# Issuing a kernel's weight loads from GpSimd instead of SyncE

## The chip, the cores and the metric

The kernel runs on one core of a Trainium2 chip. The metric is device time in microseconds (us) of one execution; the time of a version is the median of its runs. The engines are TensorE (PE in the profile; its weight loads are PEld), VectorE (DVE), ScalarE (ACT), GpSimd (POOL) and SyncE (SP). SPq and ACTq are the queues that issue DMA transfers.

## The reference

One layer of a hybrid decoder on 256 tokens of width 2048, all in float32:

```
h = rmsnorm(x) * norm_mix_w;  proj = h @ w_in            # q, k, v, z, b, a, p, g_a, g_b
q, k, v = silu(causal_conv4(q, k, v)); q, k normalised
o  = gated_delta_rule(q, k, v, decay(a), sigmoid(b))     # 16 heads of 128, chunks, triangular solve
y_a = rmsnorm(o) * silu(z);  y_b = (pool(p) - p) @ pool_w * pool_scale
x  = x + (sigmoid(g_a) * y_a + sigmoid(g_b) * y_b) @ w_out
gate, up = split(rmsnorm(x) @ w_up)                      # 2 x 5632
x  = x + (gelu(causal_conv3(gate) + b) * up) @ w_down
y  = rmsnorm(x) * norm_final_w
```

## The kernel before

Every large product is made of weight tiles: 256 rows by 512 columns of a weight matrix, which are 128 partitions x 2 x 512 floats, 512 KB. The list `srcs` holds all 530 of them in the order of their use. `w_in` and the small `pool_w` come in four groups of heads with 512 columns each, then `w_out`, `w_up` and `w_down`. The two tiles with the columns of b and a are cut otherwise, 128 x 8 x 128.

Each tile goes through three steps. `fetch` loads it into one of five raw buffers (`RAWS = 5`); `cast` on ScalarE rounds it to a short float format as `whi`; `split` on VectorE subtracts that from the raw tile and leaves the rest as `wlo`. The raw buffer is free after the split. `whi` and `wlo` have four buffers each, so three tiles can stand made ahead (`AHEAD = 3`). Then TensorE runs 12 products of 128 x 512 for the tile: eight with `whi`, four with `wlo`. The time goes through the mixer with its four groups (until about 720 us), the output projection, the up projection (about 810 to 1285) and the down projection.

Beside this main line run side chains, written as generators: turning a block (a transpose of 32 x 32 squares on VectorE into `tn`, four `flip` stores to DRAM and one load back, as `kq`, `vT`, `pu`, `gs`, `us`, `mlo` or `fhl`; `back` and `vt` are the way back for v), the decays (`rund` to `dec`, cut on GpSimd), and the inversion of a triangular matrix for each group (`cd` copied on GpSimd, `cdd` and `lb` as transfers, 31 steps on VectorE that make `tb`, then `tbd`, `tct`, the matrices `T` and `TT`, and small products into `psa`). SyncE issues all of these and all weight loads; ScalarE issues a few loads of vectors.

Nothing is scheduled by the compiler: the order on each engine is the order in which the Python program emits the instructions. A small model, `Plan`, guides it. It keeps a time for each engine (`t`, with keys PE, V, A, G, S), and `pipeline` emits the next split, cast or fetch when the model's time for the engine has come to what the step needs (`soon`). The side chains get their turns from `piece` by the same times. On the chip an engine executes in that order and waits by semaphore at each instruction; what is behind a waiting instruction on the same engine waits too. `matrices`, at the start, makes constants on GpSimd.

Of the kernel before, what the change touches and what calls it, by code (L numbers as in the profile page):

```python
# [14 lines left out]
S = 256  # L15
# [13 lines left out]
RAWS = 5  # L29


class Plan:
# [17 lines left out]
    def dma(self, eng, out):  # L50
        n = 4
        for d in out.shape:
            n *= d
        self.t[eng] = max(self.t[eng], self.base) + (0.42 if eng == "S" else 0.1)
        self.queue = max(self.queue, self.t[eng]) + n / (170e3 if out.shape[-1] <= 32 else 380e3)
        self.ready = max(self.ready, self.queue + 2.0)

# [50 lines left out]
def kernel(  # L108
# [22 lines left out]
    nc = Engines(plan, tc.nc)  # L131
# [12 lines left out]
    def nm(s):  # L144
        cnt[0] += 1
        return f"{s}_{cnt[0]}"
# [92 lines left out]
    def side():  # L239
        ready = plan.ready  # L240
        count = 0
        while True:
            step = None if piece(-99, min(taken[0] - (19 if taken[0] else 20), -3), 4.0) else pipeline()
            if step:
                step()
            elif not piece(-99, 9):
                break
            count += 1
        plan.at(ready)
        return count  # L250
# [11 lines left out]
    srcs = []  # L262
# [25 lines left out]
    free = []  # L288
# [3 lines left out]
    def soon(eng, time):  # L292
        return time <= max(now["PE"], now[eng])
# [8 lines left out]
    def fetch():  # L302
        i = len(raws)
        src = srcs[i]
        raw = wpool.tile(list(src.shape), F32, tag="raw", name=nm("raw"), bufs=RAWS)
        plan.at(free[i - RAWS] if i >= RAWS else 0.0)
        nc.sync.dma_start(raw, src)
        landed.append(plan.ready)
        raws.append(raw)

# [23 lines left out]
    def pipeline():  # L334
        i = len(made)
        if i < len(rounded) and soon("V", cast_at[i]):
            return split
        i = len(rounded)
        if i < min(len(raws), taken[0] + AHEAD) and soon("A", landed[i]):
            return cast  # L340
        i = len(raws)
        if i < min(len(srcs), len(free) + RAWS) and soon("S", free[i - RAWS] if i >= RAWS else 0.0):
            return fetch
        return None

    def weights():
        n = taken[0]
        taken[0] += 1
        side()
        for done, step in ((raws, fetch), (rounded, cast), (made, split)):  # L350
            while len(done) <= n:
                step()
        plan.at(max(cast_at[n], free[n] - 1.8))
        return made[n]
# [76 lines left out]
    for c in range(4):  # L431
        xc = mtile(c, [P, 2, 512], F32, f"x0_{c}")
        plan.at(0.0)
        nc.sync.dma_start(xc, x[0, :, c * 512 : (c + 1) * 512].rearrange("(t p) d -> p t d", p=P))
        x0.append((xc, plan.ready))
        fetch()
# [989 lines left out]
```

## Time and profile before

| what | us |
|---|---|
| median of three runs (1532.01 to 1534.3) | 1533.48 |
| profiled execution, own time | 1536.53 |
| its span, first to last instruction | 1533.5 |
| TensorE busy | 1519.9 |
| VectorE busy | 1059.4 |
| ScalarE busy | 775.4 |
| GpSimd busy | 62.5 |

The profiled execution is one more than the three runs. Busy time counts instructions and not the issuing of transfers, for which the queues' rows (SPq) stand. A TensorE row's end is modelled, and products overlap in the pipeline, so that 12 products of 390 ns each take 2.72 us.

### The profile page before, as it was taken

The page shows a single profiled execution, that of the slowest core. Times are in us where ns is not written, and L with a number is a line of the kernel's source. Part 1 is how long each engine was busy: PE and PEld are TensorE (multiplying, and loading weights), DVE is VectorE, ACT ScalarE, POOL GpSimd, SP SyncE. Part 2 cuts the span into 40 slices and gives each one's busy share as a digit, 9 for nine tenths or more (in the row PEclk, how much of TensorE's full clock was granted, in tenths as well). Part 3 has the DMA queues.
Part 4 walks back from the last instruction along what each step waited for, and adds up shares of the span by engine and source line. Part 5 has one row for each costly group of instructions (what it writes and reads, how often), then busy time and mean ns, then how long its engine had stood idle before and what let it go on. Part 6 is the DMA issues. An engine that isn't in the chain of part 4 may idle for free.

```text
span 1533.5 us, 19655 instructions
## 1 busy us (share of the span) xinstructions
PE 1519.9 (99%) x7110; PEld 1250.0 (82%) x7110; DVE 1059.4 (69%) x1525; ACT 775.4 (51%) x1023; POOL 62.5 (4%) x85
## 2 busy tenths in 40 slices
PE   9999999999999999999999999999999999999997
PEld 8887888777878887888888888888888888888886
DVE  5767878787887779885566766666666666444445
ACT  7475474466545854464455544444454444333343
POOL 1001001100010002000000000000000000000000
PEclk9999999999999999999999999999999999999999
DMA  8888975898578966974798888877887788666663
GB/s 292 224 238 219 256 243 149 206 260 256 159 178 245 288 201 167 264 230 143 228 281 270 235 255 245 258 220 242 253 248 227 237 255 240 204 193 192 220 194 108
DMA packets 399271, 346.09 MB, mean 226 GB/s; under 512 B 231190, under 2 KB 258374, under 8 KB 399174
## 3 DMA queue, kind: packets, MB, share of 16 engines
q1 hardware_dynamic: 395744, 339.32, 75.3%
q10 hardware_dynamic: 3430, 5.53, 1.1%
q8 instruction: 55, 0.90, 0.2%
q14 instruction: 42, 0.34, 0.1%
HBM read 315.40 MB, written 29.39 MB: 225 GB/s over the span
## 4 chain that ended last, share of the span: by engine, by line
PE 93%; DMA 3%; DVE 2%; issue 1%; SPq 0%; ACT 0%; POOLq 0%; POOL 0%; ACTq 0%; DVEq 0%
PE psm L94 79%; PE psa L94 8%; PE psb L94 6%; DMA raw<-in_w_in_dram 2%; DVE wlo L94 1%; DMA lb<-cdd 0%; DMA pu<-flip 0%; SPq L94 0%; DVE tmp L94 0%; ACT whi L94 0%; DVE tb L94 0%; DMA flip<-tn 0%; ACT xt L94 0%; DVE pb L94 0%; DVE tn L94 0%
## 5 line engine op out<-in xcount | busy, mean ns | idle before, releaser
L94 DVE TENSOR_TENSOR wlo<-raw,whi 128x1024 fp32r<-128x1024 f32 x524 | 635.2, 1220 | 293.1 <-ACT whi L94 291.4
L94 ACT CAST whi<-raw 128x1024 fp32r<-128x1024 f32 x526 | 549.0, 1051 | 536.9 <-PE psm L94 360.7
L94 PE MATMUL psm<-whi,xhl 128*128 128x512 f32 x1792 | 452.7, 393 | 1.4 <-ACT whi L94 1.4
L94 PEld LDWEIGHTS psm<-whi,xhl 128*128 128x128 f32 x1792 | 335.4, 188 | 71.6 <-ACT whi L94 2.2
L94 PE MATMUL psm<-whi,fhl 128*128 128x512 f32 x1408 | 347.8, 389 | 0.0
L94 PEld LDWEIGHTS psm<-whi,fhl 128*128 128x128 f32 x1408 | 264.5, 188 | 54.7
L94 PE MATMUL psm<-wlo,xhl 128*128 128x512 f32 x896 | 243.4, 394 | 0.6 <-DVE wlo L94 0.6
L94 PEld LDWEIGHTS psm<-wlo,xhl 128*128 128x128 f32 x896 | 167.4, 188 | 35.6 <-DVE wlo L94 1.1
L94 PE MATMUL psm<-wlo,fhl 128*128 128x512 f32 x704 | 188.3, 389 | 0.0
L94 PEld LDWEIGHTS psm<-wlo,fhl 128*128 128x128 f32 x704 | 132.2, 188 | 27.3
L94 PE MATMUL psm<-whi,hhi 128*128 128x512 f32 x168 | 65.4, 389 | 0.0
L94 PE MATMUL psm<-whi,hlo 128*128 128x512 f32 x168 | 65.4, 389 | 0.0
L94 ACT ACTIVATE fev<-psm,rs 128x512 f32<-128x512 f32 x44 | 27.9, 686 | 55.3 <-PE psm L94 55.3
L94 DVE STREAM_TRANSPOSE tn<-fev 128x1024 f32<-128x1024 f32 x22 | 27.4, 1244 | 32.3 <-ACT fev L94 32.1
L94 DVE SCALAR_TENSOR_TENSOR cy<-kq,cqw,cy 128x255 f32<-128x255 f32 (+2 forms) x96 | 44.5, 481 | 1.6
L94 PE MATMUL psm<-wlo,hhi 128*128 128x512 f32 x168 | 45.2, 389 | 0.0
L94 DVE SCALAR_TENSOR_TENSOR y<-gs,cfw,y 128x255 f32<-128x255 f32 x88 | 42.6, 484 | 3.1
L94 DVE TENSOR_TENSOR tmp<-lb,tb 128x248 f32<-128x248 f32 (+30 forms) x124 | 36.5, 294 | 10.1 <-DMA lb<-cdd 7.3
L94 DVE TENSOR_TENSOR tb<-tb,tmp 128x248 f32<-128x248 f32 (+30 forms) x124 | 36.9, 298 | 4.3
L94 POOL TENSOR_TENSOR rs<-ms,epsx 128x2 f32<-128x2 f32 (+1 forms) x4 | 4.2, 1062 | 822.0 <-DVE ms L94 822.0
L94 PE MATMUL psm<-whi,mhi 128*128 128x512 f32 x96 | 37.4, 389 | 0.0
L94 PE MATMUL psm<-whi,mlo 128*128 128x512 f32 x96 | 37.4, 389 | 0.0
(223 smaller groups left out, 1288.4 us busy)
## 6 DMA issues: line engine op xcount, KB each, us to landing
raw<-in_w_in_dram SPq DMA_DIRECT2D x226, 512.0 KB, 5.3
raw<-in_w_up_dram SPq DMA_DIRECT2D x176, 512.0 KB, 4.5
raw<-in_w_down_dram SPq DMA_DIRECT2D x88, 512.0 KB, 4.6
flip<-tn SPq DMA_DIRECT2D x184, 128.0 KB, 3.2
raw<-in_w_out_dram SPq DMA_DIRECT2D x32, 512.0 KB, 5.1
gs<-flip SPq DMA_DIRECT2D x11, 512.0 KB, 5.5
us<-flip SPq DMA_DIRECT2D x11, 512.0 KB, 6.2
kq<-flip SPq DMA_DIRECT2D x8, 512.0 KB, 8.2
```

What stands on the lines that cost most here:

```text
L94: r = getattr(self.eng, op)(out, *args, **kw)
```

## The change

Three lines. The model charges 1.0 us for a load on GpSimd (it was 0.1 for every engine but SyncE); a tile from the sixth on is issued by GpSimd; and a fetch is emitted when GpSimd's time, not SyncE's, has come to the moment at which its buffer is free.

```diff
@@ Plan.dma
-        self.t[eng] = max(self.t[eng], self.base) + (0.42 if eng == "S" else 0.1)
+        self.t[eng] = max(self.t[eng], self.base) + dict(S=0.42, G=1.0).get(eng, 0.1)
@@ fetch
         plan.at(free[i - RAWS] if i >= RAWS else 0.0)
-        nc.sync.dma_start(raw, src)
+        (nc.gpsimd if i >= RAWS else nc.sync).dma_start(raw, src)
@@ pipeline
-        if i < min(len(srcs), len(free) + RAWS) and soon("S", free[i - RAWS] if i >= RAWS else 0.0):
+        if i < min(len(srcs), len(free) + RAWS) and soon("G", free[i - RAWS] if i >= RAWS else 0.0):
```

SyncE before, in the second group of heads (from about 291 us on): the transfers of the inversion (`cdd`, `lb`), of a turned block (`flip`, `kq`) and of v (`back`) have weight loads (`raw`) between them and behind them.

```order
L94 DMA cdd_2725<-cd_2665 128x8x32
L94 DMA flip_2727<-tn_2709 64x16x32 x4
L94 DMA raw_2732<-in_w_in_dram 128x2x512
L94 DMA pnt_2408<-qnd_2703 128x4x1 x2
L94 DMA raw_2736<-in_w_in_dram 128x2x512
L94 DMA lb_2742<-cdd_2725 32x1024 x4
L94 DMA raw_2761<-in_w_in_dram 128x2x512
L94 DMA kq_2785<-flip_2727 128x4x256
L94 DMA back_2787<-tb_2783 128x8x32 x4
L94 DMA raw_2808<-in_w_in_dram 128x2x512
L94 DMA raw_2826<-in_w_in_dram 128x2x512
```

SyncE now at the same group: the weight loads are gone, and the way back of v has moved ahead of the inversion's transfers.

```order
L94 DMA back_2439<-tb_2414 128x8x32 x4
L94 DMA vt_2409<-back_2439 128x2x512
L94 DMA flip_2562<-tn_2542 64x16x32 x4
L94 DMA mlo_2486<-flip_2562 128x4x256
L94 DMA flip_2706<-tn_2686 64x16x32 x4
L94 DMA kq_2816<-flip_2706 128x4x256
L94 DMA qnd_2826<-qn_2799 4x256
L94 DMA cdd_2852<-cd_2792 128x8x32
L94 DMA pnt_2467<-qnd_2826 128x4x1 x2
L94 DMA dec_524_2899<-rund 128x1024
L94 DMA flip_2914<-tn_2889 64x16x32 x4
L94 DMA lb_2919<-cdd_2852 32x1024 x4
```

GpSimd before at the same group, from the last of the eight `cd` copies on: its own work alone.

```order
L94 COPY cd_2665<-ga_421_2404 32x2x64
L94 TENSOR_TENSOR nk_2406<-ssk_2405,half 128x8
L94 AFFINE_SELECT dec_529_2913<-dec_528_2912 128x512
L94 AFFINE_SELECT dec_528_2912<-dec_528_2912 128x4x128
L94 MEMSET T_3348 128x1024
L94 MEMSET TT_3349 128x1024
```

GpSimd now, from the same copy on: five weight loads stand between `nk` and the `dec` cuts, which wait for a transfer, and the next loads stand behind these.

```order
L94 COPY cd_2792<-ga_431_2463 32x2x64
L94 TENSOR_TENSOR nk_2465<-ssk_2464,half 128x8
L94 DMA raw_2824<-in_w_in_dram 128x2x512
L94 DMA raw_2844<-in_w_in_dram 128x2x512
L94 DMA raw_2887<-in_w_in_dram 128x2x512
L94 DMA raw_2938<-in_w_in_dram 128x2x512
L94 DMA raw_2944<-in_w_in_dram 128x2x512
L94 AFFINE_SELECT dec_525_2900<-dec_524_2899 128x512
L94 AFFINE_SELECT dec_524_2899<-dec_524_2899 128x4x128
L94 DMA raw_2952<-in_w_in_dram 128x2x512
L94 DMA raw_2993<-in_w_in_dram 128x2x512
```

At the start of the program GpSimd's third load stands ahead of the constants of `matrices`, and the two tiles of b and a behind them:

```order
L94 DMA raw_243<-in_w_in_dram 128x2x512
L94 MEMSET half 128x2
L94 AFFINE_SELECT mats<-ones 128x128 x2
...
L94 IOTA tio 128x16
L94 DMA raw_300<-in_w_in_dram 128x8x128
L94 DMA raw_302<-in_w_in_dram 128x8x128
L94 DMA raw_304<-in_w_in_dram 128x2x512
```

## The prediction

> **What bounds the kernel now.** I read the page first (shares by engine, the chain that ended last), then the span by stages, then every idle stretch of TensorE, and last what stood ahead of the weight loads on SyncE.
>
> ```profile
> PE 1519.9 (99%) x7110; PEld 1250.0 (82%) x7110; DVE 1059.4 (69%) x1525; ACT 775.4 (51%) x1023; POOL 62.5 (4%) x85
> ```
>
> That is busy us, share of the span and instructions of each engine; the chain's shares by engine and the stages follow.
>
> ```profile
> PE 93%; DMA 3%; DVE 2%; issue 1%; SPq 0%; ACT 0%; POOLq 0%; POOL 0%; ACTq 0%; DVEq 0%
> ```
>
> ```profile
> 128.00:298.00 170.00, 170.00 (x849) 138.41 (x846) 136.64 (x243) 95.75 (x143) 18.56 (x24) 1.00 0.77 214
> 298.00:385.00 87.00, 83.94 (x434) 68.04 (x433) 67.17 (x123) 53.63 (x91) 3.21 (x4) 1.00 0.89 257
> 385.00:400.00 15.00, 15.00 (x90) 12.64 (x89) 11.49 (x18) 6.00 (x10) 0.00 (x0) 0.90 0.56 147
> 400.00:785.00 385.00, 385.00 (x1901) 315.27 (x1901) 298.16 (x477) 198.41 (x274) 30.18 (x30) 1.00 0.75 217
> 785.00:1285.00 500.00, 500.00 (x2208) 414.35 (x2207) 335.37 (x382) 244.08 (x271) 1.64 (x1) 1.00 0.83 246
> 1510.00:1533.50 23.50, 14.93 (x66) 12.02 (x64) 12.87 (x26) 7.97 (x18) 1.86 (x2) 0.89 0.25 90
> ```
>
> A stage's row has its length, then busy us (instructions) of PE, PEld, DVE, ACT and POOL, then granted clock, DMA share and GB/s. TensorE is busy all the time from 128 to 298 and from 400 to 1285. Its idle time is 1533.5 - 1519.9 = 13.6 us, of which 23.5 - 14.93 = 8.57 us lie in the tail, where the last normalisation and the stores run, 3.06 us between 298 and 385, and the other 2 us at the start. Only the middle part can have to do with weight loads:
>
> ```profile
> 330.18 2.11 PE L94 MATMUL psm<-whi,xhl 128*128 128x512 f32 x8 [0.42 <-ACT whi L94]
> 341.23 1.20 PE L94 MATMUL psm<-wlo,xhl 128*128 128x512 f32 x4 [0.63 <-DVE wlo L94]
> 382.67 0.65 PE L94 MATMUL psa<-T,ga 64*64 64x64 f32 x8 [1.35 <-DVE T L94]
> 383.97 0.65 PE L94 MATMUL psa<-T,ga 64*64 64x64 f32 x8 [0.65 <-DVE T L94]
> ```
>
> Each row has start, duration and, in brackets, the idle time before it and who ended it. The four gaps sum to 3.05 us. From the chain come a tile of 12 products right behind the last gap, and one at full speed:
>
> ```profile
> 384.62 4.54 PE psm L94 x12
> 1505.89 2.72 PE psm L94 x12
> ```
>
> A tile takes 2.72 us, and this one took 4.54; the stage from 385 to 400 had a granted clock of 0.90. So those gaps cost another 4.54 - 2.72 = 1.82 us. Everything that faster weights could give back is 3.05 + 1.82 = 4.87 us.
>
> What made the weights late there is seen on SyncE:
>
> ```profile
> 298.94 0.39 SPq L94 DMA_DIRECT2D raw<-in_w_in_dram  x1
> 299.43 0.41 SPq L94 DMA_DIRECT2D kq<-flip  x1
> 299.94 8.86 SPq L94 DMA_DIRECT2D back<-tb  x4
> 308.89 3.07 SPq L94 DMA_DIRECT2D raw<-in_w_in_dram  x3
> ```
>
> Beside it stand a split on VectorE and, from the waits between 300 and 400 (us in total, times, longest), those of ScalarE for raw tiles:
>
> ```profile
> 300.10 1.22 DVE L94 TENSOR_TENSOR wlo<-raw,whi 128x1024 fp32r<-128x1024 f32 x1 [0.21 <-ACT whi L94]
> ACT whi L94 <- DMA raw<-in_w_in_dram: 19.3, 10, 6.7
> ```
>
> The split that ended at 301.32 freed a raw buffer, but SyncE stood 8.86 us at the four `back` transfers and issued the next weight load at 308.89, 7.6 us late. ScalarE, which rounds a tile when it has landed, waited 10 times. That is the shortage which TensorE met at 330 and 341. VectorE works in order, so its late splits also held back the steps that make `T` for the gaps at 382.
>
> **The change, part by part.** *Removed from SyncE:* the code's list of 530 weight tiles less 5 makes 525 loads; at 0.37 us each (the median below) that is 193 us of issue and every wait for a free raw buffer. It is off TensorE's path, so worth nothing by itself; what counts is that no weight load stands behind `back`, `flip` or `kq` any more. *Moved to SyncE's front:* `flip`, `back`, `lb`, `kq` and the others go out earlier, since no raw wait is ahead of them; TensorE seldom waits for them, 0.
>
> *Added to GpSimd:* 525 loads. The trace has no load on GpSimd, so I bound its price by rows.
>
> ```profile
> 131.47 4.51 POOL L94 COPY cd<-ga 32x128 f32<-32x128 f32 x8 [54.65 <-DVE ga L94]
> 136.07 1.66 POOL L94 TENSOR_TENSOR nk<-ssk,half 128x8 f32<-128x8 f32 x1
> 246.37 2.57 POOL L94 TENSOR_TENSOR ro<-ro,epsx 128x8 f32<-128x8 f32 x1 [46.18 <-DVE ro L94]
> 667.20 0.96 POOL L94 MEMSET TT<- 128x1024 f32 x1
> ```
>
> The work of a raw tile in the up projection (from 800 to 1285: count, ns least/median/most; the last row is us to landing):
>
> ```profile
> L94 ACT CAST whi<-raw x179: 1032/1055/1062, 801.5 to 1282.0; 128x1024 fp32r<-128x1024 f32 x179
> L94 DVE TENSOR_TENSOR wlo<-raw,whi x179: 1181/1221/1227, 802.6 to 1283.5; 128x1024 fp32r<-128x1024 f32 x179
> L94 SPq DMA_DIRECT2D raw<-in_w_up_dram x174: 367/368/686, 800.4 to 1262.6; - x174
> DMA to landing us min/median/max: 3.5/4.6/8.3
> ```
>
> From below it is SyncE's 0.37 us, from above GpSimd's dearest single instruction, `ro` at 2.57 us. I take 0.96 us, the row that, like a load, only writes and covers a whole 512 KB tile. GpSimd is then busy 525 x 0.96 + 62.5 = 567 us; at the upper end 1412 us. Both are under one load per 2.72 us.
>
> A raw buffer comes round every 5 x 2.72 = 13.6 us. In the up projection its own work is issue 0.96, landing 4.6, rounding 1.06, split 1.22, together 7.84 us; with 2.57 and the worst landing of 8.3 it is 13.15 us. So it always closes, and the cover is 5.8 us of time in the buffer. Behind it stand three made tiles, 8.16 us less rounding and split = 5.88 us. A load may be about 11.6 us late before TensorE stops.
>
> *Moved past GpSimd's own work.* In each of the four head groups eight `cd` copies and `nk` take 4.51 + 1.66 = 6.17 us, and loads now stand behind them: 6.17 + 7.84 = 14.0 us, 0.4 us over the round, taken from the 5.88 us. Cost 0 while that cover lasts. `ro` (2.57) and the two `T` fills (1.9) are smaller. `dec` waits for its own transfer, and the loads behind it wait too; this is a rival below. *The start:*
>
> ```profile
> 1.35 0.09 POOL L94 MEMSET half<- 128x2 f32 x1
> 5.75 0.14 POOL L94 IOTA tio<- 128x16 f32 x1
> 13.96 1.22 DVE L94 TENSOR_TENSOR wlo<-raw,whi 128x1024 fp32r<-128x1024 f32 x1
> 36.94 1.07 PE L94 MATMUL psm<-whi,xhl 128*128 128x512 f32 x4
> ```
>
> GpSimd's constants, 1.35 to 5.89, now stand behind its third load, which needs the split ending at 15.18: they end at about 15.2 + 1.0 + 4.5 = 20.7 us. Then come the two tiles cut into 512-byte rows, four times as many pieces; if the price goes by pieces, 3.8 us each. The tile behind them is out at 20.7 + 7.7 + 1.0 = 29.4, landed and rounded by 35.1, and TensorE wants it at 36.94. Cost 0, with 1.8 us to spare.
>
> *The port that GpSimd and VectorE share.*
>
> ```profile
> 667.36 0.82 DVE L94 COPY pb<-pu 128x4 f32<-128x4 f32 x1
> 667.43 1.22 DVE L94 TENSOR_TENSOR wlo<-raw,whi 128x1024 fp32r<-128x1024 f32 x1
> 669.69 0.17 DVE L94 COPY pa<-pb 128x8 f32<-128x8 f32 x1
> L94 DVE TENSOR_SCALAR y<-gs,cfw,vec 128x256 f32<-128x256 f32 x44 | 18.0, 409 | 14.3 <-DMA gs<-flip 14.3
> ```
>
> A copy of 4 elements took 0.82 us beside GpSimd's `TT` fill and ended with it (667.20 + 0.96 = 668.16); one of 8 elements took 0.17 us alone. The split beside the same fill took its usual 1.22. So copies wait for GpSimd's writes and the dominant two-input splits do not. If the 44 `y` scalings each wait a whole 0.96, VectorE gains 42 us in a stage where it is busy 335 of 500: nothing for TensorE. The Trainium skill, "SBUF — State Buffer", section "SBUF: two separate sides" (box on the "DVE blocks DMA" trap), states the other direction: while VectorE runs such a two-port copy, GpSimd cannot write its descriptors, and a load from its queue waits. No row here shows that direction. By it the sum would stay as it is, since no such row above lasts longer than 0.82 us against a cover of 5.8.
>
> *Where the bytes run.* The same bytes use the same engines, 0. The Trainium skill, "DMA: Bandwidth & Descriptors", section "Issuing engines are not separate DMA queues", speaks against the change: issuing from several engines saves only the sequencer's issue time. By that alone the sum would be 0. The rows say that here this issue time is the matter (7.6 us late at 308.89).
>
> *Around the span:* the profiled execution took 1536.53 us with a span of 1533.5. A further queue may cost there; the nearest row is the 0.98 us with which GpSimd's sequencer closes the chain, so 0 to 0.98, and I take 0.5.
>
> ```profile
> 1526.49 0.98 POOLq L1421
> ```
>
> Sum: -4.87 + 0.5 = -4.4, so 1532.2 for a profiled execution. The median of the three runs, 1533.48, lies 3.05 under the profiled one, so I forecast 1529.1.
>
> **Rivals.** (a) The stall only moves, no measurable change: from 298 to 385 the DMA engines were busy 0.89 of the time, and no byte goes away; loads that leave at once may crawl beside `lb` and `flip` as they did behind them. Against it: the loads were held before they were issued. Time 1533.5, between 1530.4 and 1536.5. (b) Slower: side transfers come late. They had the queue in one line with the loads; now weights enter whenever a buffer frees, and `lb`, `tbd` and `tct` take longer. The order of TensorE is fixed, so it waits at `psa<-T` as at 382: 1.35 + 0.65 + 1.82 = 3.8 us a time. It happens where `T` is later than its place in the order, at one group of four now; at all four it is 3 x 3.8 - 1.05 = +10.4, so 1543.9. For it speaks the one group that did so; against it the three that did not. (c) Slower: GpSimd falls more than 11.6 us behind, by `cd` and then a `dec` whose transfer is late, some 14 us say: 2.4 + 1.8 in each of four groups, -4.9 in return, so 1545.4. Between `cd` and `dec` stand four or five loads, each of which makes up 2.72 - 0.96 = 1.76 us, which speaks against it. (d) Slower: a load costs GpSimd over 2.72 us. From there GpSimd is the bound, at 3 us 525 x 0.28 = +147, about 1680. No row comes near but `ro`. (e) The shared port also blocks the splits: with 0.96 us on each of some 65 of them, VectorE would need 136.6 + 62 = 199 us for the 170 from 128 to 298, and 298 + 135 = 433 for the 385 from 400 on, +77 in all, about 1610. The split of 1.22 beside the fill speaks against it.
>
> **How the numbers follow.** About 0.2%, 3.1 us, is what a measurement of this kernel tells from no change. The forecast, with most of the 4.87 back, gets 0.40 and is likeliest; (a) 0.30; (b) 0.13; (c) 0.10; (d) 0.04; (e) 0.03. So faster 0.40, same 0.30, slower 0.30. Some 0.03 lie under 1527.5 (all of the 4.87, no 0.5, and the runs' own spread of 1.5 below the median); (d), (e) and the worse halves of (b) and (c) lie above 1546, about 0.15. The range is 1527.5 to 1546. For the forecast alone it is 1527.5 to 1530.4.
>
> **What would show it.** Right: no TensorE gap between 298 and 400, ScalarE's waits for raw tiles in the mixer stage well under the 19.3 us, GpSimd near 1 us a load, SyncE's waits for `wlo` gone. Wrong: TensorE gaps at `psa<-T` in several groups (b); gaps behind `cd` or `dec` with GpSimd never idle (c); GpSimd over 90% busy (d); splits clearly over 1.22 us (e). A clock under 1.00 in a stage where it was 1.00 would mean gaps just before it.

## The result and the profile after

The changed kernel took 1626.87 us (median of six runs, 1620.59 to 1628.72) against 1533.89 for the kernel before (six runs, 1532.01 to 1536.91). The ratio is 1.0595, with a 95% interval of 1.0581 to 1.0608: it is 6% or 93 us slower. I had forecast 1529.1, with 1546 as the upper end of the range. The profiled execution took 1628.72 us with a span of 1627.0.

From the page of the kernel after come the busy times, the chain that ended last, the DMA queues (packets, MB, share of 16 engines) and the issues (count, KB each, median us to landing):

```profile
PE 1553.8 (96%) x7110; PEld 1264.1 (78%) x7110; DVE 1055.9 (65%) x1525; ACT 773.4 (48%) x1025; POOL 450.8 (28%) x610
...
q0 software_dynamic: 75600, 275.28, 52.7%
q1 hardware_dynamic: 251408, 64.03, 18.0%
...
DMA 17%; PE 16%; DVE 8%; SPq 4%; issue 3%; ACT 0%; DVEq 0%; POOLq 0%; POOL 0%; ACTq 0%
...
flip<-tn SPq DMA_DIRECT2D x184, 128.0 KB, 6.4
```

The same two parts of the page of the kernel before:

```profile
q1 hardware_dynamic: 395744, 339.32, 75.3%
...
flip<-tn SPq DMA_DIRECT2D x184, 128.0 KB, 3.2
```

TensorE was 93% of the chain before. The chain of the kernel after could be followed back only to 839 us, so that its shares sum to about half of the span; TensorE has 16% there, transfers and VectorE together 25%. GpSimd is not the bound (28%). What has changed is a transfer that nobody moved: a `flip` store, still issued by SyncE and now without a weight load ahead of it, takes 6.4 us to land instead of 3.2. (These are medians of the stores whose landing is on record, in the up projection 33 of 88 before and 34 of 88 after.) Two queues carry the bytes now. The weights on GpSimd's queue go in packets of 275.28 MB / 75600 = 3.6 KB on average, and what is left on SyncE's in packets of 64.03 MB / 251408 = 255 bytes.

Where the time went is read from the start of the first product of the up projection (`psm<-whi,fhl`) and of the down projection (`psa<-whi,hhi`), in us:

| | first of up | first of down | span | mixer and output projection | up | down |
|---|---|---|---|---|---|---|
| before | 806.7 | 1285.4 | 1533.5 | 806.7 | 478.7 | 248.1 |
| after | 826.4 | 1369.5 | 1627.0 | 826.4 | 543.1 | 257.5 |

So 64.4 us were lost in the up projection, 19.7 before it and 9.4 behind it. The up projection by windows (length, busy us and instructions of PE, PEld, DVE, ACT and POOL, granted clock, DMA share, GB/s), before:

```profile
806.00:1285.00 479.00, 479.00 (x2115) 396.95 (x2114) 320.48 (x361) 232.10 (x251) 1.64 (x1) 1.00 0.83 245
```

and after:

```profile
826.00:1369.00 543.00, 501.48 (x2113) 406.60 (x2112) 307.16 (x349) 228.35 (x252) 129.09 (x177) 0.97 0.73 215
```

TensorE now stands idle for 543.00 - 501.48 = 41.5 us, and needs 501.48 - 479.00 = 22.5 us longer for the same products at a granted clock of 0.97. The DMA engines are less busy than before (0.73 for 0.83), so over the stage as a whole bandwidth is not short. The waits of the kernel after (us in total, times, longest) name the place:

```profile
POOL raw L94 <- DVE wlo L94: 962.9, 411, 14.5
...
DVE y L94 <- DMA gs<-flip: 107.2, 11, 12.6
DVE y L94 <- DMA us<-flip: 98.4, 11, 10.3
...
PE psm L94 <- DVE wlo L94: 45.8, 25, 4.9
```

and those of the kernel before:

```profile
DVE y L94 <- DMA us<-flip: 23.3, 11, 2.7
...
DVE y L94 <- DMA gs<-flip: 14.3, 11, 3.0
```

The up projection makes 22 turned blocks, 11 of gate (`gs`) and 11 of up (`us`). `y` on VectorE waits for each of them: 37.6 us in all before, 205.6 now. One such block, before, by the timeline (start, duration, what; the brackets give the idle time before it and who ended it):

```profile
896.34 1.24 DVE L94 STREAM_TRANSPOSE tn<-fev 128x1024 f32<-128x1024 f32 x1
...
897.60 2.76 SPq L94 DMA_DIRECT2D flip<-tn  x4
...
902.60 0.37 SPq L94 DMA_DIRECT2D us<-flip  x1
...
908.90 1.23 DVE L94 TENSOR_TENSOR y<-us,y 128x1024 f32<-128x1024 f32 x1 [2.68 <-DMA us<-flip]
```

and two blocks in a row, after:

```profile
898.74 4.05 SPq L94 DMA_DIRECT2D flip<-tn  x4
...
907.43 0.72 POOL L94 DMA_DIRECT2D raw<-in_w_up_dram  x1 [1.99 <-DVE wlo L94]
...
909.16 0.36 SPq L94 DMA_DIRECT2D gs<-flip  x1
...
914.44 0.41 DVE L94 TENSOR_SCALAR y<-gs,cfw,vec 128x256 f32<-128x256 f32 x1 [7.32 <-DMA gs<-flip]
...
917.34 0.72 POOL L94 DMA_DIRECT2D raw<-in_w_up_dram  x1 [9.18 <-DVE wlo L94]
...
924.48 5.72 DVE L94 TENSOR_TENSOR wlo<-raw,whi 128x1024 fp32r<-128x1024 f32 x5
...
924.58 2.85 SPq L94 DMA_DIRECT2D flip<-tn  x4
925.96 0.72 POOL L94 DMA_DIRECT2D raw<-in_w_up_dram  x1 [2.90 <-DVE wlo L94]
...
930.50 0.72 POOL L94 DMA_DIRECT2D raw<-in_w_up_dram  x1 [0.41 <-DVE wlo L94]
...
932.90 0.36 SPq L94 DMA_DIRECT2D us<-flip  x1
...
940.53 1.23 DVE L94 TENSOR_TENSOR y<-us,y 128x1024 f32<-128x1024 f32 x1 [10.34 <-DMA us<-flip]
...
942.95 1.20 PE L94 MATMUL psm<-wlo,fhl 128*128 128x512 f32 x4 [2.82 <-DVE wlo L94]
943.99 3.25 PE L94 MATMUL psm<-whi,fhl 128*128 128x512 f32 x8
```

Read it as a chain. From the first store of a block to its load back there were 902.60 - 897.60 = 5.0 us; now there are 909.16 - 898.74 = 10.4. VectorE has emitted five splits behind the transposition and then stands at `y`, since it works in order. The splits behind `y` are held, so no raw buffer comes free, and GpSimd issues nothing for 9.18 us. When `y` runs, the splits that were held run close together, three between its parts and then, behind the next transposition, five in 5.72 us, and five loads leave within 5 us (925.96 to 930.50). They are on the DMA engines just when the next `flip` store goes out at 924.58, whose load back leaves at 932.90, and the next `y` waits 10.34 us. That is more than the three tiles made ahead, 3 x 2.72 = 8.16 us, can cover: TensorE stops for 2.82 us, and the eight products behind the gap take 3.25 us, which took 1.98 elsewhere in this stretch. In this chain the delay of one block makes the burst that delays the next.

The trace also records every packet, with its queue, size and time, and there the collision can be counted. In the block of before, the 4096 packets of 128 bytes of the four stores ran in one go from 898.84 to 901.84. In the second block of after, 2004 of them had ended by 927.5; in the next 2.5 us only 146 ended, while 91 packets of 4096 bytes of the loads did; and the last ended at 932.22. Over the 22 blocks the stores took a median of 3.00 us from the first packet to the last before, with no packet of a load between them in 16 blocks, and 6.75 us after, with at least 69 packets of loads between them in every block. So it is the store's data that comes late, and not only the signal that it has landed.

### The profile page after: what moved, and what is told of

Its sections match the earlier page's. It is cut to its first block, busy times and chain, and to the rows that moved or that the text cites. A ratio compares the mean times of both kernels' runs of the same rounds, so it can differ in the third digit from the quotient of the medians.

```text
span 1627.0 us, 19782 instructions
## 1 busy us (share of the span) xinstructions
PE 1553.8 (96%) x7110; PEld 1264.1 (78%) x7110; DVE 1055.9 (65%) x1525; ACT 773.4 (48%) x1025; POOL 450.8 (28%) x610
## 3 DMA queue, kind: packets, MB, share of 16 engines
q0 software_dynamic: 75600, 275.28, 52.7%
q1 hardware_dynamic: 251408, 64.03, 18.0%
## 5 line engine op out<-in xcount | busy, mean ns | idle before, releaser
L94 PE MATMUL psm<-whi,fhl 128*128 128x512 f32 x1408 | 359.7, 399 | 2.6 <-ACT whi L94 2.6
L94 PEld LDWEIGHTS psm<-whi,fhl 128*128 128x128 f32 x1408 | 271.8, 193 | 61.8 <-ACT whi L94 3.0
L94 POOL DMA_DIRECT2D raw<-in_w_in_dram x221 | 161.1, 729 | 443.0 <-DVE wlo L94 306.6
L94 POOL DMA_DIRECT2D raw<-in_w_up_dram x176 | 127.5, 724 | 421.8 <-DVE wlo L94 409.6
L94 PE MATMUL psm<-wlo,fhl 128*128 128x512 f32 x704 | 196.2, 401 | 38.9 <-DVE wlo L94 38.9
L94 POOL DMA_DIRECT2D raw<-in_w_down_dram x88 | 63.7, 724 | 174.1 <-DVE wlo L94 169.5
L94 DVE TENSOR_SCALAR y<-gs,cfw,vec 128x256 f32<-128x256 f32 x44 | 18.0, 410 | 107.2 <-DMA gs<-flip 107.2
L94 DVE TENSOR_TENSOR y<-us,y 128x1024 f32<-128x1024 f32 x11 | 13.5, 1226 | 98.4 <-DMA us<-flip 98.4
L94 ACT ACTIVATE y<-y 128x1024 f32<-128x1024 f32 x11 | 11.7, 1064 | 83.0 <-DVE y L94 83.0
L94 ACT CAST hhi<-y 128x1024 fp32r<-128x1024 f32 x11 | 11.5, 1046 | 82.4 <-DVE y L94 82.4
L94 DVE TENSOR_TENSOR tmp<-lb,tb 128x248 f32<-128x248 f32 (+30 forms) x124 | 37.3, 301 | 18.7 <-DMA lb<-cdd 16.2
```

Of the source, the lines that this page charges most:

```text
L94: r = getattr(self.eng, op)(out, *args, **kw)
```

## The experiments

Four theories were held against each other. T: weights on a second queue take turns with SyncE's small stores on the same DMA engines, the stores land late, and VectorE's `y` holds the splits. O: the new order of instructions is what costs, or gains. S: it is GpSimd's own way of issuing loads. L: the late store would do no harm if the program's order left it more time. The comparisons of a batch share their chip and the runs of the kernel before on it, which took 1535.13 us for e1 to e4, 1534.49 for e5 to e8 and 1534.81 for e9. Where no number of runs is given, it is two. Each edit is shown against the kernel that the experiment starts from, before (e2, e3) or after (the others).

**e1_order: the changed order, all loads on SyncE.** `Timed(plan, "G", nc.sync)` issues on SyncE and charges the plan's time of GpSimd, so that the instructions come in the order of the kernel after.

```diff
+        self.raw = Timed(plan, "G", nc.sync)
-        (nc.gpsimd if i >= RAWS else nc.sync).dma_start(raw, src)
+        (nc.raw if i >= RAWS else nc.sync).dma_start(raw, src)
```

> The changed kernel's order on every engine, but all weight loads are issued by SyncE again. Theory T (two queues take turns on the DMA engines, the turned blocks' small stores lose, VectorE waits for them in its order): no second queue, so the stores land in about 3 us as before and the time is 1530 to 1540 us. Rival O (the new order by the new plan is at fault): as the changed kernel, about 1625 us. Rival S (loads by GpSimd are slow in themselves): 1530 to 1540, as T.

It took 1529.42 us (five runs, 1529.28 to 1529.47), ratio 0.9962 (0.9946 to 0.9977), just under the range that T gave. Its span was 1527.6, 5.9 us shorter than that of before. The stretch in which TensorE had met its gaps, by windows:

```profile
298.00:400.00 102.00, 102.00 (x509) 84.05 (x508) 80.93 (x142) 69.23 (x111) 8.28 (x12) 1.00 0.84 239
```

TensorE is busy all the time there and at full clock. So the new order alone gives back what I forecast (4.87 us; 1535.13 - 1529.42 = 5.7 here), and without a second queue. The loss belongs to the queue: 1626.87 - 1529.42 = 97 us between two kernels with the same order.

**e2_queue: the order of before, loads from the sixth on by GpSimd.**

```diff
+        self.raw = Timed(plan, "S", nc.gpsimd)
-        nc.sync.dma_start(raw, src)
+        (nc.raw if i >= RAWS else nc.sync).dma_start(raw, src)
```

> The order and plan of before, only the queue of the loads from the sixth on is GpSimd's. T: 1610 to 1635 us, the flip stores of the up projection land in about 6 us, VectorE waits about 200 us for gs and us. O: 1530 to 1540 us. S: 1610 to 1635 as T.

1638.98 us, ratio 1.0677 (1.0629 to 1.0725), 4 us above the range expected. Up projection 540.2 us; `y` waited 108.1 us for `gs` and 97.2 for `us`, almost as after. With e1 this closes the question of order against queue: the queue costs about 100 us in either order.

**e3_act: the kernel before, with the stores of turned blocks issued by ScalarE.** The weights stay on SyncE; GpSimd issues nothing.

```diff
+        self.turned = Timed(plan, "S", nc.scalar)
-            nc.sync.dma_start(dv[a], b[32 * a : ...])
+            nc.turned.dma_start(dv[a], b[32 * a : ...])
```

> The kernel of before, loads on SyncE, only the four flip stores of each turned block move to ScalarE's queue, so two queues share the engines but GpSimd issues no load. T: the stores of the up projection land later than the 2.9 us of before, 4 to 6 us, VectorE's waits at y grow beyond its 35 us, and the time is 1540 to 1600 us. S: the stores land in 2.9 us and the time is 1530 to 1540 us. O says nothing here.

1561.45 us, ratio 1.0172 (1.0125 to 1.0219). Its waits, and its page's row of issues:

```profile
ACT whi L94 <- DMA flip<-tn: 68.5, 10, 10.1
...
DVE y L94 <- DMA us<-flip: 53.9, 11, 5.5
...
DVE y L94 <- DMA gs<-flip: 44.9, 11, 5.0
```

```profile
flip<-tn ACTq DMA_DIRECT2D x184, 128.0 KB, 5.6
```

A second queue of the other kind, with no GpSimd in it, slows the same stores from 3.2 to 5.6 us. Their packets show the same stop: a median of 6.77 us from the first to the last of a block in the up projection, and between 908.0 and 909.5, for one, 184 packets of stores ended and 185 of loads. So it is the second queue, not GpSimd's way of issuing, that delays them. The harm is smaller in the up projection, where `y` waited 98.8 us and 484.2 us went by for 478.7; the mixer and the output projection lost 23.7 us, some more than in the kernel after. How much of this loss is the late landing is not shown, since the experiment changes a second thing: ScalarE now issues the stores in its own order, and its casts waited 68.5 us behind them (0.3 before).

**e4_late: the kernel after, with a plan that knows of the late stores.** From the end of the mixer on, the plan reckons 8 us instead of 2 until such a store has landed, so that `y` stands 8 or 9 splits behind the transposition instead of five.

```diff
+        self.far = 2.0
-        self.ready = max(self.ready, self.queue + 2.0)
+        self.ready = max(self.ready, self.queue + (self.far if out.shape[-1] <= 32 else 2.0))
...
+    plan.far = 8.0
```

> The changed kernel, but from the end of the mixer on the plan reckons 8 us instead of 2 from a turned block's store to its landing, so that VectorE's steps on gs and us stand 8 or 9 splits behind the transposition instead of 5. T: VectorE's waits for gs and us fall from about 185 us in the up projection to under 60, the up projection goes from 543 back to 480 to 500 us, and the time is 1560 to 1585 us (the mixer keeps its +20 us). S: loads stay late, the up projection stays at 530 to 545 us and the time at 1615 to 1630 us.

1564.68 us, ratio 1.0193 (1.0163 to 1.0223): 62 of the 93 us are back with the queues as they are after. In the up and down projections, what waited for these transfers, and how long they took (tile `flip` between 800 and 1380 us), was:

```profile
  DVE y L95: 2.2, 4
...
DMA to landing us min/median/max: 2.5/5.4/8.4
```

The same two lines of the kernel after:

```profile
  DVE y L94: 195.5, 21
...
DMA to landing us min/median/max: 2.7/6.1/13.9
```

The stores are still nearly twice as slow as the 2.9 us of before, but VectorE no longer meets them, and the up projection falls from 543.1 to 493 us. So the path to TensorE runs through the in-order wait of `y`. It does not go down to 478.7: 493.00 - 481.35 = 11.7 us of TensorE's idle time are left in it, which I did not trace further.

**e5_one: the kernel after, with the turned blocks' stores on GpSimd's queue too.** Stores and weights are then in one line again.

```diff
+        self.turned = Timed(plan, "S", nc.gpsimd)
-            nc.sync.dma_start(dv[a], b[32 * a : ...])
+            nc.turned.dma_start(dv[a], b[32 * a : ...])
```

> The changed kernel with its order, and the four flip stores of every turned block are issued by GpSimd too, so that loads and stores share one queue again, but GpSimd's. T (turns between two queues): the stores of the up projection land in about 3 to 4 us instead of 6.1, VectorE's waits at y fall from 184 us there to under 100, and the up projection takes 480 to 510 us instead of 543. S (GpSimd's queue is slow for whoever uses it): stores land in 6 us or later and the up projection stays at 540 us or more. Issuing a store of 1024 pieces may cost GpSimd more than the 0.72 us of a load, which the run shows.

1594.81 us, ratio 1.0394 (1.0358 to 1.0429); up projection 527 us. From its issues:

```profile
flip<-tn POOLq DMA_DIRECT2D x184, 128.0 KB, 4.3
...
gs<-flip SPq DMA_DIRECT2D x11, 512.0 KB, 9.6
us<-flip SPq DMA_DIRECT2D x11, 512.0 KB, 9.9
```

A block by the timeline:

```profile
906.84 3.51 POOL L94 DMA_DIRECT2D raw<-in_w_up_dram  x5
909.34 0.36 SPq L94 DMA_DIRECT2D us<-flip  x1
```

The stores were quicker again, as expected, and none of the 88 in the up projection landed after a load issued behind it (in the kernel after 13 of the 34 on record did). But the loads back, which stayed on SyncE, now took 9.6 and 9.9 us, against 3.8 and 6.4 after and 5.5 and 6.2 before. `y` waited 193.1 us, so my expectation for the stage missed. The slowness is no property of `flip`. Nor is it enough to be alone in the other queue, since the loads back were that in the kernel after too and were hardly slower there than before. In the two blocks of it shown above, the last load of weights had been issued 1.7 and 2.4 us ahead of them. Here five loads leave right behind the stores, and the load back is issued among them. The experiment also changes the stores' packets: on GpSimd's queue they make 299.41 - 275.28 = 24.13 MB in 84432 - 75600 = 8832 packets, 2.7 KB on average, and no longer 128 bytes each.

**e6_mixer, e7_up, e8_down: GpSimd's loads in one stage only.** All three have the order of e1; SyncE issues the rest.

```diff
+    ups = len(srcs)      # ahead of the tiles of w_up
+    downs = len(srcs)    # ahead of the tiles of w_down
-        (nc.gpsimd if i >= RAWS else nc.sync).dma_start(raw, src)
+        (nc.sync if i < RAWS else nc.gpsimd if i < ups else nc.raw).dma_start(raw, src)             # e6_mixer
+        (nc.sync if i < RAWS else nc.gpsimd if ups <= i < downs else nc.raw).dma_start(raw, src)    # e7_up
+        (nc.sync if i < RAWS else nc.gpsimd if i >= downs else nc.raw).dma_start(raw, src)          # e8_down
```

> The changed kernel's order; GpSimd issues the loads of w_in, pool_w and w_out alone, SyncE the others. T: the loss of the mixer alone, 826.4 - 800.8 = 26 us over the 1529.4 of the same order with all loads on SyncE, so 1550 to 1560 us, the up projection 478 us. S: the same.

> The changed kernel's order; GpSimd issues the loads of w_up alone. T: the mixer as in the order with all loads on SyncE (first up product at 800.8), the up projection 540 to 545 us, and up to 9 us behind it, since its last side chain ends late: 1590 to 1605 us. A rival by which the loss of the up projection is inherited from the mixer: about 1530 us.

> The changed kernel's order; GpSimd issues the 88 loads of w_down alone, beside which hardly a turned block is stored. T: nothing to be delayed, so no difference from the order with all loads on SyncE, 1527 to 1532 us. S: a load that GpSimd issues is late in itself, so a part of the 98 us in proportion to 88 of 525 loads, about 16 us: 1540 to 1550 us.

| | us | ratio (interval) | against e1 |
|---|---|---|---|
| e6_mixer | 1546.56 | 1.0079 (1.0059 to 1.01) | +17.1 |
| e7_up | 1596.96 | 1.0408 (1.038 to 1.0436) | +67.5 |
| e8_down | 1530.9 | 0.9981 (0.9967 to 0.9995) | +1.5 |

e7's up projection, by windows, has the loss of the kernel after almost to the microsecond:

```profile
801.00:1344.00 543.00, 500.59 (x2111) 406.60 (x2110) 308.92 (x353) 227.03 (x251) 123.97 (x171) 0.96 0.72 215
```

In the down projection nothing is turned after its first blocks, and there GpSimd issued 80 loads of 0.72 us at a price of 1.5 us in all:

```profile
L94 POOL DMA_DIRECT2D raw<-in_w_down_dram x80: 722/722/731, 1286.4 to 1493.1; - x80
```

That settles S, which asked for some 16 us here: the same loads from the same engine cost next to nothing where no small transfer that something waits for runs beside them. The three effects sum to 86 of the 97 us between e1 and the kernel after. By the spans of the profiled executions 99.4 - 83.2 = 16.2 us are missing: 9.0 in the mixer, taken up below, and 7.7 where up and down meet, which none of the three reproduces. There, in the kernel after, the last gate block is late, and TensorE stops again:

```profile
1372.41 0.41 DVE L94 TENSOR_SCALAR y<-gs,cfw,vec 128x256 f32<-128x256 f32 x1 [11.51 <-DMA gs<-flip]
...
1375.05 1.22 PE L94 MATMUL psa<-wlo,hhi 128*128 128x512 f32 x2 [3.54 <-DVE wlo L94]
```

e6 came out a little under what I expected of it. Its mixer and output projection took 817.4 us, against 826.4 in the kernel after with the same instructions there, but for the queue of the first tiles of `w_up`. So the size of the mixer's loss varies by some 9 us with the timing, and I can't give it more exactly.

**e9_light: e1 with the plan's charge for GpSimd at 0.1 instead of 1.0.** What is left of the change is that the plan does not charge SyncE for the loads.

```diff
+        self.raw = Timed(plan, "G", nc.sync)
-        self.t[eng] = max(self.t[eng], self.base) + dict(S=0.42, G=1.0).get(eng, 0.1)
+        self.t[eng] = max(self.t[eng], self.base) + (0.42 if eng == "S" else 0.1)
-        (nc.gpsimd if i >= RAWS else nc.sync).dma_start(raw, src)
+        (nc.raw if i >= RAWS else nc.sync).dma_start(raw, src)
```

> The order with all loads on SyncE once more, but the plan charges GpSimd 0.1 us for a load and not 1.0, so the only thing left of the new plan is that SyncE is not charged for the loads. If that relief makes the better order: 1527 to 1532 us, as the 1529.4 of the order with 1.0, and no TensorE gap between 298 and 400. If GpSimd's charge of 1.0 makes it: 1532 to 1537 us, as before, with gaps of some 3 us.

1529.54 us (nine runs, 1529.37 to 1529.77), ratio 0.9967 (0.9957 to 0.9977), the same as e1. So the gain of the order comes from a plan that neither charges SyncE's time for a load nor waits for it. e1 and e9 are the best versions found, 0.3 to 0.4% under the kernel before.

## Why the prediction was wrong

*The step that failed* is the one on the transfers left to SyncE: "`flip`, `back`, `lb`, `kq` and the others go out earlier, since no raw wait is ahead of them; TensorE seldom waits for them, 0." They went out no earlier to any use: they landed later. With it fell "The same bytes use the same engines, 0." The bytes were the same, but in the one queue of before the stores of a block ran with no load between them in 16 of 22 blocks, while beside a second queue they shared the engines with loads in all 22, also with loads issued later. The term should have been some +67 us in the up projection and +17 to +20 before it (e7, e6).

*Rival (b)* was right in kind, since it said that weights now enter whenever a buffer frees and that side transfers take longer. It had the wrong place and a price of +10.4: TensorE waited at `psa<-T` in two groups of the kernel after, for 3.2 us in all. I had looked for the places at which TensorE waited already, `psa<-T` in the mixer. The blocks of the up projection were worse: 22 waits of VectorE, short in the trace of before (37.6 us in 22) but each with TensorE's next weights behind it. From the rows of before I could have asked what becomes of a wait of 2.68 us at `y` when the transfer takes 5 us longer, 22 times.

*The reading of the gain* was right in size, but not by the means that I named. The gaps at 330 to 384 us and the slow tile behind them did go away (e1: 5.9 us of span, forecast 4.87), but by the order that the plan chose, with every load still on SyncE. The new order moves `back` as well, so whether the load held behind it made the gaps is not shown. In the kernel after the early issue worked too: ScalarE's waits for raw tiles between 300 and 400 us fell from 19.3 to

```profile
ACT whi L94 <- DMA raw<-in_w_in_dram: 5.7, 5, 3.1
```

yet TensorE still had gaps there (98.59 busy of 100), the longest now behind a split, 1.3 us.

*GpSimd's price* was right: I took 0.96 us a load between 0.37 and 2.57, and measured 0.72, with 0.97 as the longest, also for the two tiles that are cut into four times as many pieces, for which I had allowed 3.8. (d) is out with that. (e) is out too: the splits took a median of 1.22 us after, as before. Rival (c), `cd` and `dec`, shows in no gap of TensorE.

*The mixer's loss* fits T where I followed it, in one chain. By the timeline of the kernel after the stores that go out at 40.05 let `kq` leave at 51.31, 11.3 us later:

```profile
40.05 4.68 SPq L94 DMA_DIRECT2D flip<-tn  x4
...
51.31 0.38 SPq L94 DMA_DIRECT2D kq<-flip  x1
...
58.06 1.71 ACT L94 ACTIVATE cy<-kq,cqw 128x256 f32<-128x256 f32 x4 [6.66 <-DMA kq<-flip]
...
66.00 0.19 DVE L94 TENSOR_TENSOR glog<-lp,ea 128x32 f32<-128x32 f32 x1
...
66.33 0.60 PE L94 MATMUL psb<-mats,glog 128*16 128x128 f32 x4 [4.28 <-DVE glog L94]
```

In e1, with the same order, it left after 46.59 - 38.72 = 7.9 us:

```profile
38.72 4.05 SPq L94 DMA_DIRECT2D flip<-tn  x4
...
46.59 0.37 SPq L94 DMA_DIRECT2D kq<-flip  x1
...
52.57 1.71 ACT L94 ACTIVATE cy<-kq,cqw 128x256 f32<-128x256 f32 x4 [2.48 <-DMA kq<-flip]
...
60.25 0.19 DVE L94 TENSOR_TENSOR glog<-lp,ea 128x32 f32<-128x32 f32 x1
```

There `glog` came 5.75 us earlier, of which 1.33 were there before the stores, and TensorE did not wait for it. The remaining losses of the mixer were not taken apart.

*What stays open.* The Trainium skill, "DMA: Bandwidth & Descriptors", section "Queues, rings and completion order", says that each engine goes round between the queues that have work and changes only at the end of a packet. The packets agree with that, as far as they were counted: the stores' data stops while the loads' packets run, and in one stretch of e3 as many packets of one queue ended as of the other (184 and 185). It also agrees with a store of small pieces that is slowed by a second queue (landing in 2.9 us alone in line, 5.2 in the up projection of e3, 6.1 after) and with the load back that is slowed in its place (e5). No run varied the packet size alone, so how much the size of the loads' packets matters is not known. Also open are the rest of the mixer's loss and the 11.7 us of idle time in e4.

## What to carry to other kernels

Before you move transfers to another queue, look at what stays in the old one. Here a small store in one queue went ahead of the large loads issued behind it; beside a second queue it did not, and it was the small, waited-for transfer that paid. List who waits for it, what is queued in order behind that wait, and how many tiles cover it. If a model sets the order, change the model and the queue apart from each other: here the model's part gained 0.35%, and the queue's part lost 6%.

## What the runs showed of the hardware

- A second queue doubled the time of the small transfers in the other (median in the up projection 2.9 to 6.1 us), while the DMA engines as a whole were less busy (0.83 to 0.73). The data itself stops: the packets of a block's four stores spread over a median of 6.75 us instead of 3.00, with packets of loads between them. It needs no GpSimd: stores on ScalarE's queue beside weights on SyncE's took 5.6 us instead of 3.2.
- GpSimd's issue of a direct transfer has nearly one price, whatever it carries: 0.72 us for a 512 KB weight tile, at most 0.97 for one in four times as many pieces, 0.82 for a 128 KB store in 1024 pieces of 128 bytes (e5). SyncE took 0.37 us for a weight tile.
- After a TensorE gap of 2.82 us the next eight products took 3.25 us instead of 1.98, so a gap cost here about 1.5 times its length, as the stage as a whole shows (64.0 us lost for 41.5 idle).
